# First attention of a two-layer encoder: scores with keys on partitions instead of queries

## The chip, the cores and the metric

The kernel is one launch on one core of a Trainium2 chip, written with the Tile framework (a scheduler orders each engine's queue, pools hand out buffers). The metric is the device time of one execution in microseconds (us). The engines are named as in the profile: PE (TensorE), PEld (its weight loads), DVE (VectorE), ACT (ScalarE), POOL (GpSimd), SP (the queue that issues most DMAs).

## The reference

Two layers of an encoder on x of 1 x 1024 x 1024 in float32. Every sub-layer is an RMS norm with a shift, scale and gate worked out from a conditioning vector c (`mod = silu(c) @ ada_w[i] + ada_b[i]`, six vectors of 1024 a layer, called modulation sums below). Layer 0 mixes tokens by multi-head latent attention, layer 1 by dilated windows; each layer ends in a squared-ReLU MLP of width 4096. The change lies in layer 0's attention:

```python
q = rms_norm(concat(q_nope, rope(q_rope)), g_q)     # 16 heads, 96 wide
k = rms_norm(concat(k_nope, k_rope), g_k)
s = einsum('bqhd,bkhd->bhqk', q, k) * 96 ** -0.5    # 1024 x 1024 a head, float32
p = softmax(s, axis=-1)
o = einsum('bhqk,bkhd->bqhd', p, v)                 # v is 64 wide
x = x + gate1 * (o @ w_o)
```

## The kernel before

A product in full precision is made of parts: `split` (L110 to L113) makes a high part by an ACT copy to a rounded float32 form (L112) and a low part by a subtraction (L113, on DVE or POOL), and `mm3` (L395 to L397) adds three PE products, high x high, high x low and low x high.

`K.mla` computes layer 0's attention in stages, each with its PSUM pool. The second stage (pool psB, 8 banks; two halves of eight heads, eight token tiles each) multiplies the latents by the weights of q and of k and v, normalises, applies the rotary embedding and stores every head's q, k and v side by side in DRAM (`qkv`, L756). `prep` (from L684) loads one head back (`hraw`), transposes q and k on PE (L697, sets of four 128 x 128 transposes), and splits them into qh, ql, kh, kl with 96 rows and 1024 columns; v's high and low parts stand beside each other in `hv` (POOL, L707 and L708). Head 0 is prepared in the second half of that stage, a quarter after each of four tiles.

The third stage (pool psC) is the attention. It is unrolled over 256 steps n, four for each pair of query tiles (`unit`), four pairs for each of 16 heads. `scores` (from L776) puts 128 queries on partitions and 1024 keys on columns: six products of 512 columns into two PSUM banks (tag "s", two buffers). DVE takes the minimum of the negated scores along the row (L788), ACT the exponential with the row's sum (L789), DVE the reciprocal (L791), POOL scales the row (L792). Five steps later `transp` turns the weights round on PE, four tiles a set (L803, tag "t", three banks), and splits them (pT, ACT and DVE). Nine steps later `av` multiplies them by the values: 64 products of 256 columns a head, value parts as the weights of the array (L816). Every second pair of query tiles two ACT copies (L825, L826) and a POOL addition (L827) put 64 rows of the output together; when both heads of a pair are there, it is split for the output product (L836), and the first four pairs go to DRAM (`oTd`, L841).

Beside this a step in seven is an `ada_step`: it loads 128 x 1024 of `ada_w` (pinned in SP's order) and adds the slice loaded by the step before into an accumulator on DVE (L166, L167); after eight slices PE sums over the partitions (`ada_end`, L212, L218). Layer 0's four remaining sums run here, layer 1's first five in the first MLP (its steps 8 to 40 in the second product), the last in the second MLP. Towards the end `tail` loads and splits the first half of the output weights. `proj_res` then multiplies by the output weights; it begins six output tiles with the first six of eight 128-row groups before it needs the last two. Buffers come from a general pool of 29 (G) and a second of 19 (X, `aux(19)`), both of 128 x 1024 float32.

Of the kernel before, what the change touches and what calls it, by code (L numbers as in the profile page):

```python
# [41 lines left out]
class K:  # L42
    def __init__(self, ctx, tc, a, ng=29):
# [8 lines left out]
        self.ax = None  # L52

# [8 lines left out]
    def X(self, name, shape=(P, 1024), dt=F32R):  # L62
        return self.ap.tile(list(shape), dt, tag="x", name=self.nm(name))

# [20 lines left out]
    def setup(self):  # L85
        nc, a = self.nc, self.a
        nc.scalar.preload_act_table_set("natural_log_exp_and_others")
        self.ident = self.C("ident", [P, P])
        make_identity(nc, self.ident)
        self.ones = self.C("ones", [P, 1])  # L90
        nc.vector.memset(self.ones, 1.0)
        self.mods = {}
        self.gates = self.dp.tile([4, 1024], F32, name="gates")
        self.eps = self.C("eps", [P, 1])
        nc.vector.memset(self.eps, EPS)

# [86 lines left out]

    def pinned(self, ins):
        return self.tc.keep_in_program_order(ins)
# [14 lines left out]
    def ada_start(self, todo):  # L200

        self.ada_todo = [(l, s, j) for l, s in todo for j in range(9)]
        self.ada_cur = self.ada_store = None

    def ada_end(self, l, s, acc, row, psp, tag):

        nc = self.nc
        PS = lambda: psp.tile([P, 512], F32, tag=tag, bufs={"m": 8, "t": 3}.get(tag), name=self.nm("psac"))
# [12 lines left out]
    def ada_step(self, psp, tag):  # L221
        nc = self.nc
        store, self.ada_store = self.ada_store, None
        cur, self.ada_cur = self.ada_cur, None
        if self.ada_todo:
            l, s, j = self.ada_todo.pop(0)
            w = None
            if j < 8 or s % 3 == 2:
                w = self.X("adaw", dt=F32)
# [5 lines left out]
            self.ada_cur = (l, s, j, w)  # L235
        if store:
            self.pinned(nc.sync.dma_start(out=store[0], in_=store[1]))
        if cur:
            l, s, j, w = cur
            if j == 0:  # L240
                self.ada_acc = self.X("adacc", dt=F32)
# [267 lines left out]
    def mla(self, xs, ada0, xs1, mods, tail):  # L509
# [26 lines left out]
        with tc.tile_pool(name="psA", bufs=2, space=PSUM, reuse_waits="tile") as psp:  # L536
# [66 lines left out]
            self.pinned(nc.vector.scalar_tensor_tensor(gq, self.colc[0:QK, 133:134], -(QK ** -0.5),  # L603
# [76 lines left out]
        heads = {}  # L680

        def prep(h, part, pt):

            if part == 0:  # L684
                hd = heads[h] = {}
                src = qkv[h].rearrange("(t p) e -> p t e", p=P)
                raw = [self.load(src[:, 4 * i : 4 * i + 4, :], (P, 4, 256), "hraw") for i in range(2)]
                hd["raw"] = raw
                alloc = self.X if h == 0 else self.G
                for n in ("qh", "ql", "kh", "kl"):  # L690
                    hd[n] = alloc(n, (QK, 1024))
                hd["v"] = alloc("hv", (P, 8, 128))
            hd = heads[h]
            n, i = ("q", "q", "k", "k")[part], part % 2
# [4 lines left out]
            hi, lo = hd[n + "h"][:, sl], hd[n + "l"][:, sl]  # L699
# [5 lines left out]
            if part >= 2:  # L705
                dst, v = hd["v"][:, 4 * i : 4 * i + 4, :], hd["raw"][i][:, :, 192:256]
                nc.gpsimd.tensor_scalar(dst[..., 0:64], v, 1.0, 1.0, op0=ALU.mult, op1=ALU.mult)  # L707
                nc.gpsimd.tensor_tensor(dst[..., 64:128], v, dst[..., 0:64].bitcast(F32), op=ALU.subtract)  # L708

        with tc.tile_pool(name="psB", bufs=8, space=PSUM, reuse_waits="tile") as psp:  # L710
            B = lambda name: psp.tile([P, 512], F32, tag="b", name=self.nm(name))
            raw = None
            for hf in range(2):
                w = hw[hf]
                for t in range(NT):
# [49 lines left out]
                    elif 2 <= t < 6:  # L765
                        prep(0, t - 2, B("pqk"))
# [5 lines left out]
        with tc.tile_pool(name="psC", bufs=2, space=PSUM, reuse_waits="tile") as psp:  # L772

            def unit(h, j):
                return {"h": h, "j": j, "p": []}

            def scores(u, k):
                hd, i, b = heads[u["h"]], k // 2, k % 2
                qs = slice((2 * u["j"] + i) * P, (2 * u["j"] + i + 1) * P)
                if b == 0:  # L780
                    u["ps"] = psp.tile([P, 1024], F32, tag="s", name=self.nm("pss"))
                ks = slice(b * 512, (b + 1) * 512)
                self.mm3(u["ps"][:, ks], hd["qh"][:, qs], hd["ql"][:, qs], hd["kh"][:, ks], hd["kl"][:, ks], True, True)
                if b == 1:
                    m = self.sm("am", 1)
                    l = self.sm("al", 1)
                    p = self.G("p", dt=F32)
                    nc.vector.tensor_reduce(m, u["ps"], op=ALU.min, axis=AX.X)  # L788
                    nc.scalar.activation(p, u["ps"], AF.Exp, scale=-1.0, bias=m, accum_out=l)  # L789
                    rl = self.sm("arl", 1)  # L790
                    nc.vector.reciprocal(rl, l)  # L791
                    nc.gpsimd.tensor_scalar(p, p, rl, 1.0, op0=ALU.mult, op1=ALU.mult)  # L792
                    u["p"].append(p)

            def transp(u, b):

                i, kh = b // 2, b % 2
                if b == 0:
                    u["pT"] = [[self.G(f"pT{k}", (P, 4, 256)) for _ in range(2)] for k in range(2)]
                pt = psp.tile([P, 512], F32, tag="t", bufs=3, name=self.nm("ppt"))  # L800
                for k in range(4):
                    kt = 4 * kh + k
                    nc.tensor.transpose(pt[:, k * P : (k + 1) * P], u["p"][i][:, kt * P : (kt + 1) * P], self.ident)  # L803
                o = lambda hl: u["pT"][hl][kh][:, :, i * P : (i + 1) * P]
                self.split(o(0), o(1), pt.rearrange("p (k q) -> p k q", k=4))

            avs = {}

            def av(u, b):
                h, j = u["h"], u["j"]  # L810
                if b == 0 and j % 2 == 0:
# [1371 lines left out]
```

## Time and profile before

| what | value |
|---|---|
| three runs | 3430.1, 3431.41, 3434.76 us; median 3431.41 |
| the profiled execution, first to last instruction | 3429.9 us |
| median of the runs less that span | 1.5 us |
| busy, share of the span | PE 95%, DVE 74%, ACT 55%, POOL 22% |
| first score product, first output product | 223.88 us, 741.35 us |
| mean granted clock of PE | 0.985 |

The profile is one execution. A row of a group gives line, engine, operation, output and input tiles, shapes and count, then busy us and the mean of one in ns, then the idle time ahead of the group and what ended it. "psm" is the MLP's PSUM tile, "pss" the scores', "ppt" the transposed weights', "pav" the values' product, "pqk" the head preparation's.

### The profile page before, as it was taken

To read this page: it belongs to the slowest core of one execution; us is meant where nothing else is said; L and a number is where in the kernel's file an instruction comes from. 1 tells how busy PE (TensorE), PEld (TensorE's weight loads), DVE (VectorE), ACT (ScalarE), POOL (GpSimd) and SP (SyncE) were. 2 spreads that over 40 slices of the span, in tenths; PEclk is the share of its full clock that TensorE was granted. 3 is DMA by queue.
4 is the path that set the end of the run, shared out by engine and by line. 5 is a ranking of instruction groups with operands and counts; after the bars stand their busy time and mean duration, and the time that the engine had idled before them with its cause. 6 is when DMAs were issued, how large, how long until landed. Compare 5 with 4: busy or idle time off the path is not lost.

```text
span 3429.9 us, 55643 instructions
## 1 busy us (share of the span) xinstructions
PE 3266.5 (95%) x20054; PEld 2877.7 (84%) x20054; DVE 2528.9 (74%) x4645; ACT 1880.1 (55%) x3894; POOL 757.7 (22%) x1257
## 2 busy tenths in 40 slices
PE   6988999999999999999999989999999799999999
PEld 6877787778888787778899989998999688888887
DVE  6667778766987876786667777777788669777666
ACT  5546676653545433542257787778766445454342
POOL 6464444430111000001132232223111001110000
PEclk9999999999999999999999999999999899999999
DMA  5451221143554889534333433333343835438564
GB/s 182 132 178 62 87 100 55 68 167 111 171 194 159 290 244 339 167 119 141 111 114 109 118 101 108 111 102 98 93 130 104 227 111 172 167 140 295 194 206 133
DMA packets 379012, 506.87 MB, mean 148 GB/s; under 512 B 32517, under 2 KB 262194, under 8 KB 378730
## 3 DMA queue, kind: packets, MB, share of 16 engines
q1 hardware_dynamic: 351402, 411.93, 38.4%
q0 software_dynamic: 27328, 91.31, 7.1%
q8 instruction: 160, 2.62, 0.3%
q14 instruction: 122, 1.00, 0.1%
HBM read 371.78 MB, written 132.42 MB: 147 GB/s over the span
## 4 chain that ended last, share of the span: by engine, by line
PE 54%; DVE 4%; DMA 2%; ACT 1%; issue 1%; SPq 0%; POOL 0%; DVEq 0%; ACTq 0%; POOLq 0%
PE psm L396 7%; PE psm L397 7%; PE psm L395 7%; PE psproj L395 5%; PE psproj L396 5%; PE psproj L397 5%; PE pss L1753 2%; PE psv L397 2%; PE psv L395 2%; PE psv L396 2%; PE pspt L1779 2%; PE psq L1722 2%; PE psav L1794 2%; PE psav L1795 1%; DMA w2r<-in_mlp_w 1%
## 5 line engine op out<-in xcount | busy, mean ns | idle before, releaser
L396 PE MATMUL psm<-dl,dh 128*128 128x512 f32 x896 | 351.8, 393 | 10.4 <-DVE dl L113 10.4
L395 PE MATMUL psm<-hf,wf 128*128 128x512 f32 x896 | 349.9, 391 | 4.2 <-ACT wf L112 4.2
L397 PE MATMUL psm<-dh,dl 128*128 128x512 f32 x896 | 350.9, 392 | 0.0
L396 PE MATMUL psm<-hf,wf 128*128 128x512 f32 x896 | 349.2, 390 | 0.0
L397 PE MATMUL psm<-hf,wf 128*128 128x512 f32 x896 | 346.8, 389 | 0.0
L395 PE MATMUL psm<-dh,dh 128*128 128x512 f32 x896 | 333.9, 393 | 6.2 <-ACT dh L112 6.2
L395 PE MATMUL psproj<-wqkh,hTp 128*128 128x256 f32 x1024 | 300.5, 293 | 0.0
L397 PE MATMUL psproj<-wqkh,hTp 128*128 128x256 f32 x1024 | 292.1, 285 | 0.0
L396 PE MATMUL psproj<-wqkl,hTp 128*128 128x256 f32 x1024 | 291.5, 285 | 0.0
L112 ACT ACTIVATE dh<-ufr 128x1024 fp32r<-128x1024 f32 x112 | 118.3, 1057 | 203.7 <-PE psm L396 51.0
L396 PEld LDWEIGHTS psm<-dl,dh 128*128 128x128 f32 x896 | 169.5, 189 | 48.1 <-DVE dl L113 12.8
L395 PEld LDWEIGHTS psm<-dh,dh 128*128 128x128 f32 x896 | 168.9, 189 | 44.0 <-ACT dh L112 8.2
L792 POOL TENSOR_SCALAR p<-p,arl 128x1024 f32<-128x1024 f32 x128 | 144.9, 1132 | 271.5 <-DVE arl L791 216.4
L395 PEld LDWEIGHTS psm<-hf,wf 128*128 128x128 f32 x896 | 168.7, 188 | 40.1 <-ACT wf L112 5.3
L397 PEld LDWEIGHTS psm<-dh,dl 128*128 128x128 f32 x896 | 169.4, 189 | 35.3
L396 PEld LDWEIGHTS psm<-hf,wf 128*128 128x128 f32 x896 | 168.7, 188 | 34.8
L397 PEld LDWEIGHTS psm<-hf,wf 128*128 128x128 f32 x896 | 168.3, 188 | 35.0
L396 PEld LDWEIGHTS psproj<-wqkl,hTp 128*128 128x128 f32 x1024 | 195.7, 191 | 0.0
L395 PEld LDWEIGHTS psproj<-wqkh,hTp 128*128 128x128 f32 x1024 | 195.3, 191 | 0.0
L397 PEld LDWEIGHTS psproj<-wqkh,hTp 128*128 128x128 f32 x1024 | 195.3, 191 | 0.0
L112 ACT ACTIVATE pT<-ppt 128x512 fp32r<-128x512 f32 x256 | 144.4, 593 | 76.6 <-PE ppt L803 74.3
L113 DVE TENSOR_TENSOR dl<-ufr,dh 128x1024 fp32r<-128x1024 f32 x112 | 136.8, 1222 | 65.3 <-ACT dh L112 51.7
(389 smaller groups left out, 9528.3 us busy)
## 6 DMA issues: line engine op xcount, KB each, us to landing
ufr<-uf SPq DMA_DIRECT2D x112, 512.0 KB, 4.9
adaw<-in_ada_w SPq DMA_DIRECT2D x96, 512.0 KB, 7.2
w2r<-in_mlp_w SPq DMA_DIRECT2D x96, 512.0 KB, 4.9
w1r<-in_mlp_w SPq DMA_DIRECT2D x64, 512.0 KB, 4.4
bt<-bias SPq DMA_DIRECT2D x128, 256.0 KB, 2.9
wqkr<-in_dil_w_in SPq DMA_DIRECT2D x96, 256.0 KB, 4.1
qkv<-st SPq DMA_DIRECT2D x32, 512.0 KB, 2.9
hraw<-qkv SPq DMA_DIRECT2D x32, 512.0 KB, 6.8
```

Source lines behind the costliest of these rows:

```text
L112: nc.scalar.activation(hi, src, AF.Copy)
L113: (lo_eng or nc.vector).tensor_tensor(lo, src, hi.bitcast(F32), op=ALU.subtract)
L395: mm(out, lh, rh, start=first, stop=False)
L396: mm(out, lh, rl, start=False, stop=False)
L397: mm(out, ll, rh, start=False, stop=last)
L792: nc.gpsimd.tensor_scalar(p, p, rl, 1.0, op0=ALU.mult, op1=ALU.mult)
L1722: nc.tensor.transpose(ps[:, (2 * e + k) * P : (2 * e + k + 1) * P], s4[:, i, e, 64 * k : 64 * k + 128], identr)
L1753: nc.tensor.matmul(ps[:, e * 256 : (e + 1) * 256], q[:, e, k, :], u["k"][:, e, w0 : w0 + 256], start=k == 0, stop=k == 1)
L1779: nc.tensor.transpose(ps[:, (n * e + b) * P : (n * e + b + 1) * P], p[:, e, c : c + P], self.ident)
L1794: nc.tensor.matmul(o, pT[:, 0, c], v, start=b == 0, stop=False)
L1795: nc.tensor.matmul(o[:, 0:128], pT[:, 1, c], v[:, 0:128], start=False, stop=b == n - 1)
```

## The change

- **Scores.** Keys stand on partitions, queries on columns: one slot n is one of eight key tiles of one head, 128 slots. q is scaled by +96^-0.5 and has a 97th row with the negated maximum of each query, k a 97th row of ones, so that the first of the three products subtracts the maximum. The exponential needs no bias and no transposes follow: `weights` splits it (low part on POOL in odd slots, on DVE in even slots and in the last twelve).
- **Maxima.** `rowmax` multiplies only the high parts, queries on partitions, 16 products and 16 DVE maxima a head, spread over slots of the head before (and of the one before that) by the table `mid`; `rowstore` negates them, transposes 128 x 8 on PE, and sends the row through DRAM into row 97.
- **Sums.** v's high part gets two columns of ones, so that row 64 of the product holds the softmax sums. They go through DRAM (`lrow`), are inverted on 128 x 8 (`recip`), and come back over 64 partitions (`rrow`, `rl`); POOL multiplies (`finish`), and every second head is split (`spread`).
- **Fixed slots.** What runs in which slot is written out by hand, and `pin_from` keeps every engine's queue of this stage in program order.
- **Preparation.** k goes first, then q; heads 0 and 1 are prepared in the stage before, as are head 0's maxima and its row; head h from the fourth slot of head h-2 on.
- **Modulation.** An `ada_step` in slots 1, 3 and 5 of every eight, loads two steps ahead; layer 1's scale sum (1, 1) is made here too, and the first MLP's steps begin at 16 instead of 8. X has 16 buffers instead of 19; after the attention a pool of three serves the modulation steps. The output weights' loads are at slots 117 to 123.

```diff
+    def pin_from(self, mark):
+        bb = self.nc.cur_bb.bb.instructions
+        last = {}
+        for n, i in enumerate(bb):
+            prev, last[i.engine] = last.get(i.engine), i
+            if n >= mark and prev is not None:
+                self.tc.add_manual_dep(i, prev.name, mybir.DependencyInfo(
+                    mybir.DependencyClass.NoSync, mybir.DependencyReason.DATA), reason="pin_from")
...
+        cur = self.ada_cur.pop(0) if len(self.ada_cur) == ahead or not self.ada_todo and self.ada_cur else None
...
             if part == 0:
+                for n in ("kh", "kl", "qh", "ql"):
+                    hd[n] = self.G(n, (QK + 1, 1024))
+                nc.sync.dma_start(out=hd["kh"][QK : QK + 1, :].bitcast(F32), in_=self.onerow)
+                hd["v"] = self.mp.tile([P, 1040], F32R, tag="hv", bufs=3, name=self.nm("hv"))
+            n, i = ("k", "k", "q", "q")[part], part % 2
...
+                if i == 1:
+                    nc.gpsimd.memset(vh[:, :, 64:66].bitcast(F32), 1.0)
...
+        def rowmax(h, j, b, ps):
...
+            nc.tensor.matmul(ps, hd["qh"][0:QK, j * P : (j + 1) * P], hd["kh"][0:QK, b * 512 : (b + 1) * 512],
+                             start=True, stop=True)
+            nc.vector.tensor_reduce(maxes[h][:, 2 * j + b : 2 * j + b + 1], ps, op=ALU.max, axis=AX.X)
+
+        def rowstore(h, ps):
+            nm = self.sm("nm", 8)
+            nc.vector.tensor_reduce(nm, maxes.pop(h).rearrange("p (j b) -> p j b", b=2), op=ALU.max, axis=AX.X, negate=True)
+            nc.tensor.transpose(ps[0:8, 0:P], nm, self.ident)
+            mr = self.T("mr", (8, P), F32R)
+            nc.scalar.activation(mr, ps[0:8, 0:P], AF.Copy)
+            nc.sync.dma_start(out=md[h].rearrange("(t p) -> t p", p=P), in_=mr.bitcast(F32))
+            nc.sync.dma_start(out=heads[h]["qh"][QK : QK + 1, :].bitcast(F32), in_=md[h : h + 1, :])
...
-                    elif 2 <= t < 6:
-                        prep(0, t - 2, B("pqk"))
+                    else:
+                        if t in (1, 3, 7):
+                            prep_load(t // 2 if t < 7 else 2)
+                        if t in (2, 3):
+                            for i in range(2):
+                                prep(0, 2 * t - 4 + i, B("pqk"))
+                        elif t > 3:
+                            for j in ((), (0, 1, 2), (3, 4, 5), (6, 7), ())[t - 3]:
+                                [rowmax(0, j, b, B("pmx")) for b in range(2)]
+                            prep(1, t - 4, B("pqk"))
+                            if t == 6:
+                                rowstore(0, B("pmt"))
...
+            PT = lambda name: psp.tile([P, 512], F32, tag="t", name=self.nm(name))
...
+            def scores(n):
...
+                for b in range(2):
+                    qs, o = slice(b * 512, (b + 1) * 512), ps[:, b * 512 : (b + 1) * 512]
+                    nc.tensor.matmul(o, hd["kh"][:, ks], hd["qh"][:, qs], start=True, stop=False)
+                    nc.tensor.matmul(o, hd["kh"][0:QK, ks], hd["ql"][0:QK, qs], start=False, stop=False)
+                    nc.tensor.matmul(o, hd["kl"][0:QK, ks], hd["qh"][0:QK, qs], start=False, stop=True)
+                    if b == 0:
+                        between(n)
...
+            def weights(n, ps):
+                p, ph, pl = self.G("p", dt=F32), self.G("ph"), self.G("pl")
+                nc.scalar.activation(p, ps, AF.Exp)
+                self.split(ph, pl, p, nc.gpsimd if n % 2 and n < N - 12 else None)
...
+            def av(n):
...
+                for b, ps in enumerate(ps_av[h]):
+                    qs = slice(b * 512, (b + 1) * 512)
+                    nc.tensor.matmul(ps[0:66, :], vh[:, kt, :], ph[:, qs], start=kt == 0, stop=False)
+                    nc.tensor.matmul(ps[0:64, :], vl[:, kt, :], ph[:, qs], start=False, stop=False)
+                    nc.tensor.matmul(ps[0:66, :], vh[:, kt, :], pl[:, qs], start=False, stop=kt == 7)
+                    if b == 0:
+                        between(n + 2)
...
+            for h in range(1, H):
+                if h > 2:
+                    put(8 * h - 16, prep_load, h)
+                if h > 1:
+                    for i in range(4):
+                        put(8 * h - 13 + i, lambda h, i: prep(h, i, PT("pqk")), h, i)
+                for j, m in enumerate((10, 9, 9, 8, 7, 7, 6, 5)):
+                    for b in range(2):
+                        put(j // 2 if h == 1 else 8 * h - m, lambda h, j, b: rowmax(h, j, b, PT("pmx")), h, j, b, to=mid)
+                put(8 * h - 4, lambda h: rowstore(h, PT("pmt")), h, to=late)
+            for h in range(H):
+                put(8 * h + 9, evict, h, to=end)
+                put(8 * h + 12, recip, h)
+                put(8 * h + 14, finish, h)
+                if h % 2:
+                    put(8 * h + 16, spread, h, to=end)
+            mark = len(nc.cur_bb.bb.instructions)
+            for n in range(N + 17):
...
+                if n < N:
+                    ps = scores(n)
+                if len(mid.get(n, ())) > 2:
+                    between(n)
+                if 0 <= n - 2 < N:
+                    av(n - 2)
+                while mid.get(n):
+                    between(n)
+                for f in late.pop(n, ()):
+                    f()
+                if n < N:
+                    weights(n, ps)
+                for f in end.pop(n, ()):
+                    f()
+                if n % 8 in (1, 3, 5):
+                    self.ada_step(psp, "t", 2)
+            self.pin_from(mark)
...
-        k.aux(19)
+        k.aux(16)
...
-        k.ada_start([(0, s) for s in (2, 4, 3, 5)])
+        k.ada_start([(0, s) for s in (2, 4, 3, 5)] + [(1, 1)])
...
+        k.zp = zctx.enter_context(tc.tile_pool(name="ada", bufs=3, reuse_waits="tile"))
...
-            fill = [[k.ada_step] if 8 <= n < 41 else [] for n in range(56)]
+            fill = [[k.ada_step] if 16 <= n < 41 else [] for n in range(56)]
```

More of the change, by code (lines that the diff above doesn't have):

```diff
@@ L679, in mla, with prep_load @@
         hw = [w0, []]
-        heads = {}
+        heads, maxes = {}, {}
+        md, ld, rd = (self.dp.tile([H, S], F32, name=x) for x in ("mrow", "lrow", "rrow"))
+        def prep_load(h):
+            src = qkv[h].rearrange("(t p) e -> p t e", p=P)
+            heads[h] = {"raw": [self.load(src[:, 4 * i : 4 * i + 4, :], (P, 4, 256), "hraw") for i in range(2)]}
         def prep(h, part, pt):
+            hd = heads[h]
             if part == 0:
[L685 to L694, printed above, removed]
+                for n in ("kh", "kl", "qh", "ql"):
[3 more added lines that the diff above has]
+            n, i = ("k", "k", "q", "q")[part], part % 2
             o = 0 if n == "q" else 96
@@ L795, in transp @@
[L795 to L805, printed above, removed]
```

188 lines of the change are left out of this document (101 added, 87 removed).

## The prediction

> **What bounds the kernel now.** The page's head and the busy times in the stretch from the first score product (223.88 us) to the first output product (741.35 us) come first; the columns of the second row are length, then busy time (and instructions) of PE, PE's weight loads, DVE, ACT, POOL, clock, DMA.
>
> ```profile
> span 3429.9 us, 55643 instructions
> 223.88:741.35 517.47, 474.08 (x3097) 407.35 (x3097) 409.05 (x623) 361.39 (x653) 240.47 (x247) 0.99 0.25 88
> ```
>
> PE is the engine nearest to full, yet 43.4 us of the 517.5 are idle on it. What PE waited for in this stretch, longest first (total, times, longest):
>
> ```profile
> PE ppt L803 <- DVE pT L113: 17.3, 28, 1.5
> PE pss L395 <- ACT p L789: 8.6, 15, 1.4
> PE ppt L803 <- DVE ql L702: 8.6, 11, 0.8
> PE pss L395 <- DVE st L747: 4.7, 1, 4.7
> ```
>
> So the stage is PE work threaded through a round trip: scores, DVE maximum, ACT exponential, transposes, split on ACT and DVE, weighted sum. What the change removes of PE's work are these two groups (busy us, mean ns):
>
> ```profile
> L816 PE MATMUL pav<-pT,hv 128*128 128x256 f32 x1024 | 168.9, 295 | 4.2 <-DVE pT L113 2.8 <-ACT pT L112 0.9
> L803 PE MATMUL ppt<-ident,p 128*128 128x128 f32 x1024 | 148.3, 275 | 27.7 <-DVE pT L113 17.3 <-DVE ql L702 8.6 <-DVE tabp L1276 1.4
> ```
>
> A record's length includes the way through the array; what a product costs in a dense run is the spacing of starts. Six score products in order, then a set of four transposes (rows between left out):
>
> ```profile
> 408.46 0.40 PE L395 MATMUL pss<-kh,qh 96*128 96x512 f32 x1
> ...
> 409.61 0.39 PE L397 MATMUL pss<-kh,ql 96*128 96x512 f32 x1
> ...
> 412.11 0.60 PE L697 MATMUL pqk<-ident,hraw 128*96 128x128 f32 x4
> 412.46 0.37 PE L816 MATMUL pav<-pT,hv 128*128 128x256 f32 x1
> ```
>
> Five spacings in 1.15 us: 0.23 us a product of 512 columns. A set of four transposes: 0.35 us, 0.45 with the switch back, which I take as an estimate.
>
> **PE's new floor.** A slot is one of a head's eight key tiles: 6 score products, 6 products with the values, two or four maximum products in six slots of eight. Scores and values are 16 x 8 x 12 = 1536 products x 0.23 = 353.3 us. The 97th row and the 66 columns of values add no moving columns, so I cost them at nothing. Maxima of heads 1 to 15: 240 x 0.23 = 55.2. Head preparation: heads 2 to 15, 14 x 4 x 0.45 = 25.2. Row transposes: 15 x 0.25 = 3.8 (below one set of four). The products of the modulation sums stay, and a fifth sum joins:
>
> ```profile
> L212 PE MATMUL psac<-adacc,ones 128*1 128x512 f32 x8 | 3.9, 591 | 0.0
> L218 PE MATMUL psac<-ones,adacc 128*128 128x1 f32 x32 | 3.9, 251 | 0.7 <-DVE ql L702 0.7
> ```
>
> 7.8 us with the way through counted; I take 5. Together 442.5 us, 27.8 in a full head. By itself that would save 75 us of the 517.5; the rest of the sum is how much of it waits take back.
>
> **The other engines, for one head.** Rows of the same kind of work (out<-in, count, busy us, mean ns):
>
> ```profile
> L788 DVE TENSOR_REDUCE am<-pss 128x1 f32<-128x1024 f32 x128 | 155.5, 1215 | 11.7 <-PE pss L397 11.2 <-DVE arl L791 0.3
> L1701 DVE TENSOR_REDUCE dms<-dsq 128x8 f32<-128x512 f32 x96 | 65.1, 678 | 7.4 <-ACT dsq L1700 7.1
> L113 DVE TENSOR_TENSOR pT<-ppt,pT 128x512 fp32r<-128x512 f32 x256 | 167.4, 681 | 22.6 <-ACT pT L112 22.0
> L113 DVE TENSOR_TENSOR dl<-ufr,dh 128x1024 fp32r<-128x1024 f32 x112 | 136.8, 1222 | 65.3 <-ACT dh L112 51.7 <-issue 9.0 <-PE psm L396 3.2
> L702 DVE SCALAR_TENSOR_TENSOR ql<-pqk,gq,qh 96x512 fp32r<-96x512 f32 x32 | 23.7, 742 | 37.3 <-ACT qh L701 37.3
> L167 DVE SCALAR_TENSOR_TENSOR adacc<-adaw,cond,adacc 128x1024 f32<-128x1024 f32 x28 | 36.6, 1307 | 2.2 <-DMA adaw<-in_ada_w 2.2
> L789 ACT ACTIVATE p<-pss,am 128x1024 f32<-128x1024 f32 x128 | 142.4, 1113 | 31.0 <-DVE am L788 19.1 <-issue 9.4 <-ACT pT L112 1.0
> L112 ACT ACTIVATE dh<-ufr 128x1024 fp32r<-128x1024 f32 x112 | 118.3, 1057 | 203.7 <-PE psm L396 51.0 <-DMA ufr<-uf 46.8 <-PE psm L397 40.9
> L112 ACT ACTIVATE pT<-ppt 128x512 fp32r<-128x512 f32 x256 | 144.4, 593 | 76.6 <-PE ppt L803 74.3 <-POOL p L792 0.7 <-issue 0.4
> L792 POOL TENSOR_SCALAR p<-p,arl 128x1024 f32<-128x1024 f32 x128 | 144.9, 1132 | 271.5 <-DVE arl L791 216.4 <-PE pqk L697 36.3 <-PE ppt L803 7.9
> L113 POOL TENSOR_TENSOR oT<-O,oT 128x512 fp32r<-128x512 f32 x15 | 19.4, 1291 | 0.0
> L708 POOL TENSOR_TENSOR hv<-hraw,hv 128x256 fp32r<-128x256 f32 x30 | 21.9, 751 | 0.0
> ```
>
> DVE: 16 maxima x 0.68 (the row with 512 columns, and near half of the 1215) = 10.9; four low parts of the weights x 1.22 = 4.9; low parts of k and q 2 x 0.68 + 2 x 0.74 = 2.8; 40 modulation steps over 16 heads x 1.31 = 3.3; small ones 0.3: 22.2 us. ACT: 8 x (1.11 + 1.06) = 17.4, preparation 2.5, eviction 1.2 (even heads) or 2.4 (odd, which copy the row of sums apart), half a pair's split 0.6, row 0.3: about 22.5. POOL: four low parts; from 0.75 at 256 columns to 1.29 at 512 is 0.54 for 256 more, so 2.4 at 1024 (below by 1.29, above by twice that, 2.6) = 9.6; with the values' parts 2.3, normalisation 2.6 and split 1.3, 15.8. None reaches PE's 27.8.
>
> **Where waits come back.** The queues are in order and fixed, and maxima, preparation and row transposes share two PSUM banks. [...] (1) In the second slot four maxima want two banks while DVE still forms the low part of the slot before: 0.4 us. (2) In the fifth slot ACT's copy of the row of maxima stands ahead of that slot's exponential, which so starts 1.7 us late; the low part on DVE waits for it, the low parts of q queue behind, and the two maxima of the seventh slot wait for their banks: 1.2. (3) After an odd head the longer eviction delays ACT and the bank of the third slot's preparation: 0.9. That is 1.6 for even heads and 2.5 for odd, 2.1 on the mean.
>
> Then there is contention, seen each way in this trace (POOL's group stands above, 1.13 a piece):
>
> ```profile
> 568.40 2.08 POOL L792 TENSOR_SCALAR p<-p,arl 128x1024 f32<-128x1024 f32 x1
> 568.16 1.33 DVE L167 SCALAR_TENSOR_TENSOR adacc<-adaw,cond,adacc 128x1024 f32<-128x1024 f32 x1
> 696.00 1.42 POOL L708 TENSOR_TENSOR hv<-hraw,hv 128x256 fp32r<-128x256 f32 x2
> 696.66 1.85 DVE L167 SCALAR_TENSOR_TENSOR adacc<-adaw,cond,adacc 128x1024 f32<-128x1024 f32 x1
> ```
>
> At 568.40 POOL's operation met DVE's with 1.09 us of it left and grew by 0.95 over its mean of 1.13; at 696.66 DVE's met POOL's with 0.76 left and grew by 0.54 over its mean of 1.31. Overlap is mostly lost to the later one. After the change POOL is busy over half of each head, and the modulation steps fall where POOL forms the low part of an odd slot: DVE waits up to 1.6 us in the third slot, and the low part of the seventh meets the normalisation, 1.2. At worst PE sees 2.2 a head more; nothing if POOL is late. I take 0.6, nearer to nothing, since in most slots the later one is POOL, which has room. Waits 2.7 a head, x 15 = 40.5 us; both ends, 0.8 and 4.9.
>
> [...]
>
> **Its two ends.** The switch from the stage before:
>
> ```profile
> 223.88 0.77 PE L395 MATMUL pss<-kh,qh 96*128 96x512 f32 x1 [4.72 <-DVE st L747]
> ...
> 224.87 0.63 PE L397 MATMUL pss<-kh,ql 96*128 96x512 f32 x1
> 225.29 0.63 PE L395 MATMUL pss<-kh,qh 96*128 96x512 f32 x1
> ```
>
> After that gap twelve products come 0.42 apart: 2.4 us stay. The first four slots hold all of head 1's maxima, four each: DVE 2.7 + 1.2 against PE's 3.7 at most, 4 us more. At the end the last exponential, copy and low part (1.1 + 1.1 + 1.2) stand with 1.4 us of products: 3 with hand-overs. The last head's sums then make four DMA trips in series, some 18 us with their engine steps; but 18 of the 24 products of an output tile don't need them, and with six tiles begun ahead that is 24.8 us of work. I cost this at nothing, at up to 8 if a weight load stands ahead of a trip in SP's queue. Attention: 442.5 + 40.5 + 6.4 + 3 = 492.4, 25.1 less.
>
> **The stage before** gets head 0's maxima (16 x 0.23 = 3.7) and head 1's preparation (1.8). Its DVE has little room:
>
> ```profile
> 202.00:208.00 6.00, 6.00 (x34) 5.43 (x33) 4.65 (x11) 3.13 (x9) 5.17 (x15) 1.00 0.31 105
> ```
>
> Two rounds get six maxima, 4.1 us each, on 4.65 of 6; the row transpose stands ahead of the last round's products and waits for the last maximum, 3.5; the drain is 2 longer. In all 11 (6 to 15).
>
> **The row trip.** A head's eight small DMAs (sums out, back, their reciprocals out, back over 64 partitions, maxima out, back into row 97 of q, ones into row 97 of k) all go through SP, each waiting for the one before; the loads behind them are due two slots later or more. Rows (KB, us to landing):
>
> ```profile
> S<-stat SPq DMA_DIRECT2D x1, 128.0 KB, 2.1
> adaw<-in_ada_w SPq DMA_DIRECT2D x96, 512.0 KB, 7.2
> ```
>
> The reciprocal is done 3.3 us into the fifth slot; its trip, that of the maxima out and that of the row back follow in series, 3 x 2.1, so the row is there 9.6 us into it, and the next head starts after about 16. So nothing, unless a trip takes over 4.2.
>
> **Modulation sums in the first MLP.** Eight loads and nine DVE steps leave the stretch before this one:
>
> ```profile
> 1320.60 0.80 PE L395 MATMUL psm<-dh,dh 128*128 128x512 f32 x1 [5.31 <-ACT dh L112]
> 1300.00:1350.00 50.00, 44.69 (x197) 36.75 (x196) 32.48 (x35) 16.50 (x16) 1.64 (x3) 0.93 1.01 306
> ```
>
> DMA is full there, so fewer loads should shorten the 5.3 us; three fewer buffers for everything else (16 for 19) speak against. I take 3 less, between 5 less and 5 more.
>
> **Sum**: 3429.9 - 25.1 + 11 - 3 = 3412.8 of span; the median of the runs stands 1.5 above the span, so **3414 us**.
>
> **Rivals.** (a) The slack absorbs the waits: 0.8 a head, 28 less, 3386. For it: only DVE has no spare room at single places. Against: PE already loses 34.5 us to hand-overs of this kind (three rows of the first waits). (b) The gain is eaten by waits of 3.8 a head: 3431, no change. (c) Slower: DVE paces. [...] With all meetings at full price a head takes 32.2 us, not 30.5: waits 4.4, 66 in all, 3414 + 25.5 = 3440. It decides from 31.7 us a head on. (d) The row trip is late: trips of 6 us make it 21.3 after the fifth slot's start, 5.3 late, 15 x 5.3 = 80, 3494; the 7.2 us loads in the same queues speak for it, the 2.1 against.
>
> **How the numbers follow.** Forecast (3400 to 3424) 0.42, (a) 0.18, (b) 0.15, (c) 0.21, (d) 0.04. This measurement tells 0.2%, 6.9 us, from no change: faster 0.60, same 0.15, slower 0.25. Range 3380 to 3448.
>
> **What would show it.** Right: PE spacing 0.23 in scores and values; 30 to 31 us between first scores of heads; PE's waits on maxima's banks behind low parts; a first score near 235. Wrong: scores waiting for the row's DMA (d); adacc and pl on DVE stretched beyond 1.6 with PE idle behind them (c); idle under 1 us a head (a).

## The result, and the profile after

The changed kernel takes 3442.9 us (median of 7 runs, 3438.85 to 3446.91) where the kernel before takes 3434.76 beside it: 1.0027 of before, with a 95% interval of 1.0017 to 1.0038. The forecast was 3414, 17 us faster; it is 8 us slower. The time is that of rival (c), 3440, but what follows shows that its mechanism is not what decided.

Before's median is another one on each chip (3434.76 here, 3431.58, 3431.42 and 3426.89 beside the experiments), so kernels are compared by their ratio to the kernel before on the same chip, and spans only stage by stage.

First the busy times at the head of the page, before:

```profile
PE 3266.5 (95%) x20054; PEld 2877.7 (84%) x20054; DVE 2528.9 (74%) x4645; ACT 1880.1 (55%) x3894; POOL 757.7 (22%) x1257
```

and changed:

```profile
span 3439.2 us, 53091 instructions
...
PE 3293.4 (96%) x19046; PEld 2797.8 (81%) x19046; DVE 2493.0 (72%) x4491; ACT 1857.3 (54%) x3638; POOL 788.8 (23%) x1205
```

PE runs 1008 products fewer than before (19046 for 20054) and is busy 27 us longer. That is the first oddity: the change takes work from PE, and PE's busy time grows. Cut into stages (from one first product to the next, us):

| stage | before | changed | difference | forecast |
|---|---|---|---|---|
| up to the first score product | 223.9 | 236.8 | +12.9 | +11 |
| attention, to the first output product | 517.5 | 498.4 | -19.1 | -25.1 |
| output product of layer 0 | 92.85 | 92.1 | -0.75 | 0 |
| first MLP, first product (hf, wf) | 314.2 | 319.2 | +5.0 | } -3 |
| first MLP, second product (dh, dl) | 338.4 | 335.7 | -2.7 | } |
| layer 1's values (psv) | 242.0 | 245.4 | +3.4 | 0 |
| layer 1's attention and output product | 1073.4 | 1075.3 | +1.9 | 0 |
| second MLP, first product (hf, wf) | 310.4 | 318.9 | +8.5 | 0 |
| second MLP, second product and end | 317.3 | 317.4 | +0.1 | 0 |

Ahead of the first output product the kernel gains 6.2 us. Behind it, where the forecast had 3 us less, it loses 15.5, most of it in products that the change does not touch. The same 200 us of the second MLP in both kernels (length, then busy time and instructions of PE, weight loads, DVE, ACT, POOL, then clock and DMA), before:

```profile
2850.00:3050.00 200.00, 200.00 (x885) 165.59 (x883) 155.93 (x253) 98.80 (x169) 32.77 (x48) 1.00 0.49 173
```

and changed:

```profile
2850.00:3050.00 200.00, 200.00 (x863) 162.11 (x862) 153.17 (x248) 97.89 (x169) 31.57 (x46) 1.00 0.47 169
```

PE is busy for all of the 200 us in both, at the full clock, waiting for nothing; it gets through 22 instructions fewer. So the products themselves are slower. A stretch of them, before:

```profile
2899.72 0.39 PE L395 MATMUL psm<-hf,wf 128*128 128x512 f32 x1
2899.95 0.39 PE L396 MATMUL psm<-hf,wf 128*128 128x512 f32 x1
2900.17 0.39 PE L397 MATMUL psm<-hf,wf 128*128 128x512 f32 x1
...
2901.31 0.39 PE L396 MATMUL psm<-hf,wf 128*128 128x512 f32 x1
```

and changed:

```profile
2899.63 0.39 PE L414 MATMUL psm<-hf,wf 128*128 128x512 f32 x1
2899.86 0.40 PE L415 MATMUL psm<-hf,wf 128*128 128x512 f32 x1
2900.09 0.40 PE L413 MATMUL psm<-hf,wf 128*128 128x512 f32 x1
...
2901.26 0.39 PE L415 MATMUL psm<-hf,wf 128*128 128x512 f32 x1
```

Seven spacings take 1.59 us before and 1.63 after. Over all 1344 products of this group in the second MLP the mean spacing (those under 0.25 us) is 226.7 ns before and 231.9 after; in the first MLP 226.7 and 232.5, in layer 1's values 226.8 and 230.1. The groups dh and dl of the MLPs' second products stay at 227. No row of waits shows this: it is in the length of work, in stages that the prediction took for unchanged.

Inside the attention (from the first score product to the first output product) PE is idle for 26.2 us:

```profile
236.80:735.20 498.40, 472.15 (x2072) 321.49 (x2073) 366.06 (x451) 334.70 (x390) 266.26 (x184) 0.98 0.31 101
```

Its waits (total, times, longest):

```profile
PE pqk L717 <- DVE mx L744: 13.1, 13, 1.2
PE pmx L742 <- DVE mx L744: 4.8, 11, 0.6
PE pss L841 <- ACT p L855: 3.9, 1, 3.9
...
PE pmx L742 <- DVE ql L722: 2.3, 13, 0.2
```

So 26.2 us remain where there were 43.4. None is for the row's DMAs. Half of them are one wait: the preparation in the third slot of a head, for a bank that a maximum holds, 13 times 1.0. What holds the maximum up:

```profile
401.05 2.39 POOL L121 TENSOR_TENSOR pl<-p,ph 128x1024 fp32r<-128x1024 f32 x1
...
401.42 3.11 DVE L175 SCALAR_TENSOR_TENSOR adacc<-adaw,cond,adacc 128x1024 f32<-128x1024 f32 x1
...
404.45 1.27 DVE L744 TENSOR_REDUCE mx<-pmx 128x1 f32<-128x512 f32 x2
...
405.18 0.64 PE L717 MATMUL pqk<-ident,hraw 128*96 128x128 f32 x4 [1.14 <-DVE mx L744]
```

The modulation step of the second slot starts 0.37 us after POOL's low part has started, ends 1.09 us after that has ended, and takes 3.11 us for an operation of 1.27. Two maxima stand behind it in DVE's queue, and PE behind them. It happens in each of 14 heads (2.77 to 3.14 us); the group's mean says the same:

```profile
L175 DVE SCALAR_TENSOR_TENSOR adacc<-adaw,cond,adacc 128x1024 f32<-128x1024 f32 x35 | 68.0, 1943 | 0.0
```

A step that meets nothing takes 1.274 us on the mean; 35 of them would be 44.6 us, and 23.4 are stand-still.

### The profile page after: what moved, and what is told of

It is laid out like the page before. It is cut to its first block, busy times and chain, and to the rows that moved or that the text cites. A ratio compares the mean times of both kernels' runs of the same rounds, so it can differ in the third digit from the quotient of the medians.

```text
span 3439.2 us, 53091 instructions
## 1 busy us (share of the span) xinstructions
PE 3293.4 (96%) x19046; PEld 2797.8 (81%) x19046; DVE 2493.0 (72%) x4491; ACT 1857.3 (54%) x3638; POOL 788.8 (23%) x1205
## 4 chain that ended last, share of the span: by engine, by line
PE 81%; DVE 7%; DMA 3%; ACT 3%; issue 2%; POOL 1%; SPq 0%; DVEq 0%; ACTq 0%; POOLq 0%
PE psm L414 11%; PE psm L415 11%; PE psm L413 11%; PE psproj L413 5%; PE psproj L415 5%; PE psproj L414 5%; PE pss L1862 2%; PE psv L415 2%; PE psv L413 2%; PE psv L414 2%; PE pspt L1888 2%; PE psy L413 2%; PE psy L415 2%; PE psy L414 2%; PE psq L1831 2%
## 5 line engine op out<-in xcount | busy, mean ns | idle before, releaser
L413 PE MATMUL psm<-hf,wf 128*128 128x512 f32 x896 | 354.6, 396 | 2.6 <-ACT wf L120 2.6
L414 PE MATMUL psm<-hf,wf 128*128 128x512 f32 x896 | 353.9, 395 | 0.0
L415 PE MATMUL psm<-hf,wf 128*128 128x512 f32 x896 | 351.7, 395 | 0.0
L744 DVE TENSOR_REDUCE mx<-pmx 128x1 f32<-128x512 f32 x256 | 170.8, 685 | 37.4 <-PE pmx L742 37.4
L121 POOL TENSOR_TENSOR pl<-p,ph 128x1024 fp32r<-128x1024 f32 x58 | 145.6, 2511 | 183.9 <-ACT ph L120 182.5
```

The source lines that it names most:

```text
L121: (lo_eng or nc.vector).tensor_tensor(lo, src, hi.bitcast(F32), op=ALU.subtract)
L413: mm(out, lh, rh, start=first, stop=False)
L414: mm(out, lh, rl, start=False, stop=False)
L415: mm(out, ll, rh, start=False, stop=last)
L744: nc.vector.tensor_reduce(maxes[h][:, 2 * j + b : 2 * j + b + 1], ps, op=ALU.max, axis=AX.X)
```

## The experiments

Two questions. **What slows products that were not changed?** Theory 1: their place in SBUF. One line of the diff, which neither the excerpt nor the prediction spoke of, takes two small buffers away from layer 1's merge:

```diff
-            f, w = (self.sm(x, 48)[:, 0 : 6 * n] for x in ("mgf", "mgw"))
+            f, w = (self.sm(x, 48, bufs=4)[:, 0 : 6 * n] for x in ("mgf", "mgw"))
```

Six buffers of 192 bytes become four, so the tiles behind them (the second pool, X) begin 384 bytes lower in every partition: at byte 146944 in place of 147328, by the built programs' allocations. The general pool stays at 18048. Modulo 256 both were 128; now X is at 0. Products whose moving columns (hf) lie in one pool and whose weights (wf) in the other are the slow ones; those with both in X (dh, dl) are not. Theory 2: something that runs beside them. **What holds the attention at 498 us?** Theory A: DVE's step standing beside POOL. Theory B: DVE has no room wherever the step is.

**128 bytes ahead of the second pool (`pad128`).**

```diff
+        pp = ctx.enter_context(tc.tile_pool(name="pad", bufs=1))
+        nc.vector.memset(pp.tile([P, 32], F32, name="pad"), 0.0)
         k.aux(16)
```

> The changed kernel with 128 unused bytes a partition put ahead of the second pool, nothing else. Theory 1 (place): the changed kernel's small tiles take 384 bytes less, so its second pool begins at byte 146944 of a partition instead of 147328, while the general pool stays at 18048; a product whose moving columns lie in the one pool and whose next weights lie in the other then starts its successor after 232.5 ns instead of 226.7, because the two offsets no longer agree modulo 256 bytes. With 128 bytes in between (147072) they agree again: products of the two MLPs (hf, wf) back at 0.227 us, 20 us less than the changed kernel: 0.9965 to 0.998 of before. Theory 2 (company): the slower products come from what runs beside them since the change, and the place is chance: 1.0027 of before, products at 0.232.

Measured: 1.0012 (1.0003 to 1.0021). The products of both MLPs are back at 226.8 and 226.7 ns, the values' at 226.8, and the part behind the first output product takes 2690.6 us for 2704.0. But the first score is at 245.1 instead of 236.8. DVE's queue in the first 24 us:

```profile
22.64 0.09 DVE L2159 MEMSET pad<- 128x32 f32 x1 [17.67 <-SPq L1455]
```

The clearing of the pad waits 17.67 us there for a load in SP's queue, with the first stage's steps queued behind it. The spacings speak for theory 1; the total has a cost of the experiment's own in it, which the next but one takes away.

**64 bytes (`pad64`)**, the same edit with 16 columns.

> The changed kernel with 64 unused bytes ahead of the second pool (147008). Theory 1 with a rule of 256 bytes: offsets differ by 192 modulo 256, products of the MLPs stay at 0.232 and the time at 1.002 to 1.003 of before. Theory 1 with a rule of 64 bytes: as fast as with 128 bytes, 0.9965. Theory 2: 1.0027.

Measured: 1.0033 (1.0021 to 1.0045), with the same 8 us at the front (first score 245.0). The spacing in the MLPs is 228.8, between the two:

```profile
2850.00:3050.00 200.00, 200.00 (x876) 164.30 (x875) 157.06 (x250) 99.22 (x168) 30.76 (x45) 1.00 0.47 165
```

876 instructions, for 885 and 863. Neither form of the rule in the expectation fits: 64 bytes off is not as bad as 128 off, and not as good as none.

**The bytes reserved and never written (`room`).**

```diff
         self.sp = ctx.enter_context(tc.tile_pool(name="small", bufs=4))
+        self.sp.tile([P, 32], F32, tag="pad", bufs=1, name="pad")
```

> The changed kernel with 128 bytes a partition reserved among the small tiles and never written, so that only the place of the second pool changes (147072 instead of 146944). Theory 1 (place): the clearing of the 128 bytes, which stood ahead of the first stage in DVE's queue in the earlier run and put the first score at 245.1, is what cost 8 us there; without it the first score is back at 237, the products of the MLPs stay at 0.227, and the time is 13 to 20 us under the changed kernel: 0.997 to 0.999 of before. Rival: moving the pool itself costs the 8 us at the front, and the time stays at 1.001.

Measured: 0.9989 (0.998 to 0.9998), 3428.0 us. No instruction differs from the changed kernel; a pool lies 128 bytes higher, and the same 200 us of the second MLP read as before the change:

```profile
2850.00:3050.00 200.00, 200.00 (x885) 165.58 (x884) 155.73 (x253) 99.19 (x170) 32.88 (x48) 1.00 0.48 171
```

The first score is at 239.4 and the part behind the first output product takes 2687.6: 16.4 us less than in the changed kernel, and 1 less than before the change.

**The kernel before, moved by 32 bytes (`before_room32`)**, the same edit with 8 columns in the kernel before.

> The kernel before with 32 bytes a partition reserved among its small tiles and never written: its second pool begins at 147360 instead of 147328, nothing else changes. Theory 1 (place): products of the MLPs start 0.2327 us apart instead of 0.2267, and 20 us come on top: 1.006 of before, without the 8 us at the front that the cleared bytes cost. Theory 2 (company): 1.000.

Measured: 1.0061 (1.0047 to 1.0075), 3445.95 us. Nothing of the change is in it, and it is slower than the changed kernel:

```profile
2850.00:3050.00 200.00, 200.00 (x859) 161.05 (x858) 151.93 (x245) 97.94 (x168) 30.78 (x45) 1.00 0.49 170
```

Spacing 232.7 in both MLPs. Theory 2 is out from both sides: the slow products come with the place alone, in either kernel. The changed kernel's own trace agrees: of the spacings of hf and wf in its two MLPs, 108 fall where DVE, ACT and POOL have nothing in hand, and their mean is 232.4 ns; 1906 fall where DVE is busy throughout, at 232.2.

The same 32 bytes were also put ahead of the second pool and cleared there, as in `pad128` (`before_pad32`; theory 1 said 1.006, theory 2 1.000). Measured: 1.0086 (1.0072 to 1.01). The spacing is 232.7 again, and the first score is at 231.9 instead of 222.6 in `before_room32`: the clearing's cost comes on top.

**The maxima left out (`nomax`)**, on `room`.

```diff
+                if h:
+                    nc.vector.memset(maxes[h], 0.0)
+            if h:
+                return
...
-                nc.scalar.activation(p, ps, AF.Exp)
+                nc.scalar.activation(p, ps, AF.Exp, scale=0.05)
```

> As the kernel with 128 bytes reserved, without the products and DVE maxima of heads 1 to 15 (240 of each): their row is zero, and the exponential takes 0.05 of the score so that it stays finite; it prices the maxima and leaves part of the softmax out. Theory A (PE sets the pace, and what waits there are come from maxima): 240 x 0.2325 = 56 us of products and some 20 us of waits behind DVE's maxima go, the attention takes 498 - 76 = 422 us or a little more, 0.975 of before. Theory B (DVE sets the pace): it falls by 240 x 0.68 = 163 us of DVE work as far as PE's other work allows, to PE's floor of 16 x 96 products and preparation, 390 us. Theory C (the row's trip or ACT sets the pace): under 30 us less.

Measured: 0.9769 (0.9754 to 0.9784). The attention in `room`, then here:

```profile
239.40:739.20 499.80, 473.56 (x2072) 322.72 (x2073) 365.78 (x451) 334.77 (x390) 266.19 (x184) 0.98 0.30 99
```

```profile
239.80:659.10 419.30, 403.76 (x1831) 278.01 (x1832) 210.84 (x225) 330.16 (x390) 270.55 (x187) 0.99 0.36 118
```

419.3 us against 499.8: 80.5 less, where theory A said 76, B 110 and C under 30. So PE sets the pace and the row trip does not. The maxima cost their 56 us of products and 24.5 around them, of which 10.7 are idle time of PE (26.2 in `room`, 15.5 here) and some 5 each are spacings of 0.25 to 0.35 us and time at half clock.

**The steps in even slots (`even`)**, with the cleared pad.

```diff
-                if n % 8 in (1, 3, 5):
+                if n % 8 in (0, 2, 4):
```

> The changed kernel with 128 unused bytes ahead of the second pool, and the modulation steps in slots 0, 2 and 4 of eight instead of 1, 3 and 5. Theory A (SBUF is shared): in the second slot of a head DVE's modulation step stands still while POOL forms its low part (3.1 us at 401.42 in the changed kernel where one takes 1.3), and the third slot's preparation waits 1.17 us a head for maxima behind it; in even slots POOL has no low part in hand, the step takes 1.3 everywhere and 10 to 15 us go: 0.993 to 0.994 of before. Theory B: the step is late anyway, whichever slot it is in, because DVE itself has no room ahead of the third slot: under 4 us less than with the 128 bytes alone.

Measured: 1.014 (1.0125 to 1.0156), 0.013 (43 us) more than `pad128`: the gain of theory A did not come, and neither had foreseen the size. PE's waits in the attention:

```profile
PE pmx L742 <- DVE mx L744: 30.8, 27, 2.2
PE pmx L742 <- DVE ql L722: 13.5, 14, 1.4
PE pmx L742 <- DVE kl L121: 7.8, 10, 0.9
```

The stand-still beside the low part is gone (the step's mean is 1.49, not 1.94), but in even slots DVE has its own low part, and the step behind it stands ahead of the second slot's four maxima. In every second head it also meets POOL's split of the output:

```profile
347.36 4.06 POOL L121 TENSOR_TENSOR oT<-O,oT 128x512 fp32r<-128x512 f32 x2 [2.91 <-ACT oT L120]
...
348.00 2.31 DVE L175 SCALAR_TENSOR_TENSOR adacc<-adaw,cond,adacc 128x1024 f32<-128x1024 f32 x1
```

**Slots 3, 4 and 5 (`s345`)**, the same line with (3, 4, 5), on `room`.

> As the kernel with 128 bytes reserved, and the modulation steps in slots 3, 4 and 5 of eight instead of 1, 3 and 5. Theory A: the 15 us that the third slot's preparation waits come from the step in the second slot alone, which DVE holds for 3.1 us beside POOL's low part while four maxima are due; slots 4 and 5 have no maxima and take the step without a wait behind it: 10 to 15 us less than with the reserved bytes alone, 0.993 to 0.995 of before. Theory B: DVE is short of room wherever the step is put, as in the even slots: 5 to 30 us more.

Measured: 1.0017 (1.0008 to 1.0026), 10 us more than `room` beside it (3438.19 for 3428.0) and within the 5 to 30 of theory B. The third slot lasts 3.61 us instead of 4.82, as A had it, and the time comes back elsewhere:

```profile
PE pmx L743 <- DVE ql L723: 10.5, 9, 1.5
PE pss L842 <- ACT p L856: 6.0, 1, 6.0
...
PE pqk L718 <- DVE adaw L232: 4.8, 2, 2.4
PE psac L237 <- DVE adacc L176: 4.2, 1, 4.2
```

Maxima wait for banks that the low part of q holds, and the last head, with its sums due there, is 8.6 us longer (37.3 from its first score to the first output product, for 28.7). Some 40 us of this attention pass at half clock, for 20.5 in `room`.

**The scale sum back in the MLP (`mlpada`)**, on `room`.

```diff
-        k.ada_start([(0, s) for s in (2, 4, 3, 5)] + [(1, 1)])
+        k.ada_start([(0, s) for s in (2, 4, 3, 5)])
...
-        k.ada_start([(1, s) for s in (0, 2, 4, 3)])
+        k.ada_start([(1, s) for s in (1, 0, 2, 4, 3)])
...
-            fill = [[k.ada_step] if 16 <= n < 41 else [] for n in range(56)]
+            fill = [[k.ada_step] if 8 <= n < 41 else [] for n in range(56)]
```

> As the kernel with 128 bytes reserved, with layer 1's scale sum made in the first MLP again and that MLP's modulation steps begun at 8 instead of 16. By the prediction's steps: eight loads more in the first MLP cost 3 us there (its waits for the second product's forms 15.7 us again, not 12.5), and eight steps fewer in the attention save the stand-still of 2 to 3 heads, 3 us: the time is that of the kernel with the bytes reserved, within 3 us. Rival: the MLP does not notice the loads (its gain came from the place of the pools or from the fewer buffers), and the time falls by 3 to 9 us.

Measured: 0.9983 (0.9974 to 0.9992), 0.8 us under `room`. The attention takes 496.7 us for 499.8, and the second product of the first MLP 342.7 for 339.7: a trade of 3 for 3, as the prediction's steps had it. Some 1.7 of the attention's 3 us are less time at half clock (17.1 us for 20.5), so the price of the steps is not shown so closely. The MLP's waits for forms do not carry it, though (7.1 + 6.5 + 0.7 + 0.4 us, against 6.5 + 7.8 + 0.7 in `room`); where in that product the 3 us arise stays open.

**Fewer steps in the second slot (`s35`)**, on `mlpada`, whose 36 steps fit.

```diff
-                if n % 8 in (1, 3, 5):
+                if n % 8 in (3, 5) or n % 8 == 1 and n < 33:
```

> As the kernel with 128 bytes reserved and layer 1's scale sum in the first MLP (attention 496.7 us, 0.9983 of before), with the 36 modulation steps of the attention in slots 3 and 5 of every head, and in slot 1 of the first four heads alone. Theory A (the step in the second slot costs 1.17 us a head because it stands still beside POOL's low part): the third slot's wait goes in some nine heads, 10 us, and the heads at the end, which had no steps, pay some 3 for theirs: 7 us less, 0.996. Theory B (DVE's room is used up, a wait taken away here comes back there, as with slots 3, 4 and 5): within 3 us of 0.9983.

Measured: 0.9979 (0.9971 to 0.9988), by the ratio within B's 3 us of `mlpada`. But the attention takes 489.4 us for 496.7, the 7 us of theory A, and its waits went where A said (PE idle for 18.0 us, for 25.7). The first row is `mlpada`:

```profile
PE pqk L718 <- DVE mx L745: 11.9, 12, 1.2
```

and the second `s35`:

```profile
PE pqk L718 <- DVE mx L745: 2.9, 3, 1.2
```

Three of these waits are left, one for each step of a second slot that stood still (2.8 to 3.1 us). The ratio alone cannot settle it: the intervals overlap, and what follows the first output product takes from 2685.9 to 2691.7 us in the profiles with 128 bytes reserved.

**The low parts of two slots exchanged (`swap`)**, on `room`.

```diff
-                self.split(ph, pl, p, nc.gpsimd if n % 2 and n < N - 12 else None)
+                self.split(ph, pl, p, nc.gpsimd if n % 8 in (0, 3, 5, 7) and n < N - 12 else None)
```

> As the kernel with 128 bytes reserved (0.9989), with the low part of the first slot of a head on POOL and that of the second on DVE, instead of the other way round; the work of each engine in a head is the same, the modulation steps stay in slots 1, 3 and 5. Theory A (sharing of SBUF): POOL has nothing in hand when DVE makes the second slot's step, which takes 1.3 us instead of 3.1, and the third slot's preparation waits 1.17 us less in each of 13 heads: 10 to 15 us less, 0.995 to 0.996. Theory B: DVE makes its low part in the second slot just ahead of the step, and the maxima come as late as before: between 3 us less and 5 more.

Measured: 1.0003 (0.9995 to 1.0012), nothing gained, by the ratio 5 us more than `room`, the end of theory B. And yet only two of 35 steps still lose over 0.2 us (23.4 us of stand-still became 3.1). What stands now, in every second head:

```profile
400.91 2.54 POOL L122 TENSOR_TENSOR oT<-O,oT 128x512 fp32r<-128x512 f32 x2
...
402.26 2.28 DVE L122 TENSOR_TENSOR pl<-p,ph 128x1024 fp32r<-128x1024 f32 x1
```

DVE's own low part (1.22 us undisturbed) takes 2.28 beside POOL's split of the output, and the third slot's preparation waits 1.65 us in those heads (2.25 once) and some 0.5 in the others, for 1.17 and 0.86 in `room`. The exchange moved the meeting from one two-input operation of DVE to another.

**Both (`s35swap`).**

> Both edits: the scale sum back in the first MLP, steps in slots 3 and 5, the low parts of the first two slots exchanged. Theory A: where there is no step in the second slot there is nothing left to gain from the exchange, so the time is that of the kernel with the steps alone, 0.996, and 2 to 3 us less from the first four heads. Theory B: 0.998 to 1.000.

Measured: 0.9966 (0.9953 to 0.9978), 3415.05 us for 3426.89, and 4 us under `s35` on the same chip (3419.07). No step loses over 0.14 us (28 steps, mean 1.28). But the attention takes 490.4 us for 489.4 in `s35`, with some 3 us more of it at half clock, so the traces do not show that the exchange brought the 4 us, and where they arise stays open. This version is faster than both kernels: the change with 128 bytes reserved, the scale sum left in the MLP, steps in the second slot of the first four heads alone, and the low parts of a head's first two slots exchanged.

## Why the prediction was wrong

**The step that failed is the sum's silent term**: that stages behind the attention keep their time, but for 3 us in the first MLP. They took 16.4 us more by the place of a pool (2704.0 against 2687.6 in `room`). Of the 26.4 us between the forecast span of 3412.8 and the measured 3439.2 that is the largest part; 2 are the 3 us less that did not come, 6.0 the attention's and 1.9 the stage before. It follows from a line of the diff that has nothing to do with the attention, and that no sum of this prediction's kind, instructions times a length, would have priced. The profile of before could not show it, since its two pools lay in the fast place.

Had the place been kept, the kernel would still have gained only what `room` shows, 0.11% instead of 0.5%. `room`'s span is 14.0 above the forecast one, in three terms:

- **The stage before**: first score at 239.4 for a forecast 234.9, 4.5 more. In the changed kernel itself it was 236.8; the seven kernels here with the same front and nothing cleared lie between 234.8 and 239.8. There the stage grew by 12.9 us, within the 6 to 15 and a little over the 11. The row transpose (`pmt`) waits 2.6 us for the last maximum, for a forecast 3.5.
- **Attention**: 499.8 for a forecast 492.4 (498.4 in the changed kernel, which spends 3.5 us less of it at half clock).
  - PE's floor was right: 1776 products at a mean 0.2326 us (413.1), preparation 20.7, transposes of the row 1.5 and sums 8.7 make 444.0, for 442.5. That it came so near is part luck: the products took 4.6 us more than forecast and the preparation 4.5 less (0.37 us a set, for an estimated 0.45).
  - What PE loses beside it is 54.4 us in the changed kernel, for a forecast 49.9 (40.5 + 6.4 + 3). Its parts are others: 26.2 are idle time in the profile, some 8.5 are two stretches at half clock (10.2 and 6.8 us long), and some 12 are gaps of about 90 ns, 133 spacings of 0.25 to 0.35 us; some 8 are not accounted for.
  - The three places of waiting fared unequally, and no run shows their terms (0.4, 1.2 and 0.9) as the prediction had them; from the start of a maximum's product to its maximum it is 0.44 us here (400.37 to 400.81). The bank in the second slot, 0.4, cost PE nothing after the first head. The seventh slot's wait, 1.2, came to 0.2 (2.3 us in 13 heads). The third slot's preparation waited in 13 heads and not in odd ones alone, 0.8 to 1.2 us, because of the step that stood still. For contention the prediction took 0.6 of a possible 2.2, since in most slots the later one would be POOL; in the second slot it was DVE's step, in 14 of 14 heads, and that wait alone is 1.0.
- **Behind**: 1 less than before the change, for a forecast 3; profiles with the same bytes differ here by 6.

**Rival (c)** priced the meetings of DVE and POOL, the right two partners, and its sign was there (steps of 3.1 us with PE waiting behind them). It came within 3 us of the measured time, but by luck, for that reason did not decide: heads follow each other in 31.1 us (first scores of heads 1 and 15 at 270.2 and 706.2), under the 31.7 from which it was to decide, and with the place restored its stage is 17.7 us shorter than before the change, not longer. **Rival (d)** is out: in no profile here does PE wait for the row. **Rival (a)**, 0.8 us a head (464 for the attention), was never near; the shortest attention here, with the maxima in it, is 489.4.

## What to carry to other kernels

When stages that a change does not touch get slower at full PE and full clock, compare the spacing of starts in a dense run, then the addresses of the tiles: a small buffer more or less shifts the pools behind it (here by 384 bytes, and 16.4 us came with them). Before timing a change, look where its pools begin, and reserve bytes so that they begin where they did.
A wait that one operation causes is not a sum that comes back when it is moved: in `swap` 23.4 us of stand-still became 3.1 and the time did not fall, since DVE's low part stood in the step's stead (2.28 us for 1.22). Take it out of the place, or find a place where neither its own engine nor its partner has work.

## What the runs showed of the hardware

- **In the MLPs' products of 128 x 128 weights and 512 columns the spacing goes with the place of the second pool.** Where the moving columns lie in the one pool and the next product's weights in the other, it is 226.7 ns with the second pool at 147328 (all 2662 spacings of the kernel before), 226.8 at 147072 (2661 pairs of `pad128`), 228.9 at 147008 (2386 pairs of `pad64`), 232.7 at 146944 (2388 pairs of the changed kernel) and 233.3 at 147360 (2391 pairs of the kernel before with 32 bytes). Pairs of the changed kernel with both in the general pool stay at 227.5 (268 pairs). The difference between the two places, modulo 256 bytes, is 0 in the first two of these, then 64, 128 and 224. The two with difference 0 lie 256 bytes apart themselves, and the slow 146944 lies 128 below the second; that the spacing repeats every 256 bytes is an estimate from these five places, and no other was tried. Whether it is the next product's weights or its own that count, these pairs do not tell, since both lie in the same pool, and no trace shows what makes the product slower.
- In the attention that relation does not show: by the allocations scores have both operands at difference 0, and they lie at 234.4 ns (231 before the change); the products with the values lie at 230 to 232 in the changed kernel and in `room` alike, although the values lie 128 bytes higher there. Why was not tried.
- **An operation of DVE with two inputs in SBUF took longer beside one of POOL's; one that reads PSUM hardly did.** In the changed kernel's attention, a modulation step or a low part of the weights that starts while POOL has over 0.3 us left of an operation on two tiles ends 1.08 to 1.09 us after that: 14 of 14 steps (2.77 to 3.14 us, for 1.28 with POOL idle) and 11 of 11 low parts (1.42 to 2.29 us, for 1.22). In `swap` a low part takes 2.28 beside POOL's split. The maxima, which read PSUM alone, took 0.685 us on the mean behind such an operation (126 of them, none over 0.693) and 0.686 with POOL idle; the low parts of k and q, with one input in PSUM, 0.681 and 0.747 for 0.677 and 0.741. The other way round, POOL's low part took 2.64 to 2.90 us where it started during such a step or low part of DVE, for 2.39 alone. "Sharing of SBUF" is theory A's name for this; the traces show the lengths and the ends.
- A clearing of 128 bytes put the first score at 245.1; where the same bytes were reserved and not cleared it was at 234.8 to 239.8. The trace shows the clearing's wait of 17.67 us in DVE's queue, with the first stage's steps behind it.
